# A 3x3 convolution with 2x2 maximum pooling: one five-product step becomes a four-product step, in a new written order

## The chip, the cores and the metric

The kernel runs on one core of a Trainium2 chip. The time is that of one execution on the device, in microseconds (us), as the median of several runs. TensorE multiplies, VectorE (DVE) and ScalarE (ACT) work on the accumulators, GpSimd (POOL) adds and subtracts rows in the on-chip memory, and SyncE (SP) issues loads and stores.

## The reference

The input x is 16 images of 64 channels with 64 x 64 pixels, the weight 128 x 64 x 3 x 3, all float32. The image is padded by one zero pixel on each side, convolved, and each 2 x 2 block of the result is reduced to its maximum:

```python
x_pad = np.pad(x, ((0, 0), (0, 0), (pad, pad), (pad, pad)), mode='constant')
conv[b, co] += weight[co, ci, kh, kw] * x_pad[b, ci, kh:kh+h, kw:kw+w]   # over ci, kh, kw
output[b, c, i, j] = np.max(conv[b, c, i*pool_size:(i+1)*pool_size, j*pool_size:(j+1)*pool_size])
```

The output is 16 x 128 x 32 x 32. Because only the maximum of each pair of rows is kept, the two rows of a pair may be computed with shared products.

## The kernel before

Two images are put on the 128 partitions, 64 channels each. So there are eight image pairs, and each is cut into four chunks of 16 rows: 32 steps. A step makes eight pooled rows for both images. Its two halves are called h = 0 and h = 1 (lower and upper 64 partitions); their matmuls have 64 rows each and are issued alternately, so that two run at the same time.

A step is of one of two kinds, set by the string SEQ.

- A K step works on bf16 rows (tile kx). It has five products of three matmuls each (one for each column of the filter): PAa and PAb for the even row of a pair in one accumulator, PBa and PBb for the odd row in another, and PR, the middle filter row over the sum of both rows (tile ks, made on VectorE by the entry KS), which is common to both. After PAb, ScalarE copies the first accumulator out (EV), VectorE takes the maximum into the second (MX), PR is added after that, ScalarE copies the odd columns out (OD), and VectorE takes the maximum with the even columns (CM). Its rows arrive as bf16 by a casting load on GpSimd's queue (entries L0 to L5, two steps each). The first two K steps are loaded in float32 instead (kfirst and ksecond) and cast on VectorE (XO, XE) and ScalarE (X1, X2).
- A W step works on float32 rows (tile wx, loaded by SyncE, entries LD.i). It has four products on combinations of rows: we (entry E on VectorE or e on GpSimd), wz (Z, GpSimd), wy (Y, GpSimd) and ws (S, VectorE), used by P2, P0, P3 and P1. P2 makes an accumulator, ScalarE writes its negative into a second one (SE), P0 adds to the first and P3 to the second; then copy (ev), maximum (mx), P1, and od and cm as above.

A K step so has 30 matmuls and a W step 24. Before, there are 14 K steps and 18 W steps.

The order of all of it is written out by hand in the string ORDER, one token for each instruction group, and the engines take their instructions in that order. A token such as P2.0.0+P0.1.1 (a product entry) issues the three matmuls of two products alternately. The accumulators are four banks for each half, given out first come, first served (`take`). A sum on GpSimd is made to wait for the last sum on VectorE that stands before it in ORDER (`on_gpsimd`). At the start, the weights are combined into 28 slots (D2, D0, GM, GP on VectorE, g0 to g2 copies on ScalarE, GS on GpSimd), transposed by TensorE in groups of four (TD2 and so on, line 174) and copied out (VD2 and so on, lines 185 to 191). TGM, TGP and their copies VGM, VGP serve the W steps. The first use of a bank that held transposed weights needs a matmul with zeros (line 155).

SyncE issues loads and stores in order; a store waits for its cm or CM. The last two steps in SEQ are stored by halves, the others whole.

Of the kernel before, what the change touches and what calls it, by code (L numbers as in the profile page):

```python
# [11 lines left out]
def kernel(  # L12
# [295 lines left out]
    stored = {}  # L308

    def colmax(c, i, h):  # L310
        g = (c, i, h)
# [3 lines left out]
        nc.vector.tensor_tensor(  # L315
            out=o[:, h], in0=acc[h][tb[g]][:, :, 0::2], in1=od.pop(g), op=MAX
        )
# [4 lines left out]
        n = order_of.index((c, i))
        stored[c, i] = stored.get((c, i), 0) + 1
        if n >= len(order_of) - 2:
            nc.sync.dma_start(out=dst[:, h], in_=src[:, h])
# [53 lines left out]


    ORDER = """
        D2 g0 D0 g1 TD2 KX2 g2 TD0 GS VD2 TG0 TG2 VG0 TG1 XO VD0 VG2 PAa.0.0+PAa.0.1 GM XE PAb.0.0+PAb.0.1
# [4 lines left out]
        SE.1.0 Y.1 P1.0.0+P0.1.1 MX.1.1 P0.1.0+P1.0.1 MX.1.0 ev.1.1 P3.1.0+P3.1.1 KS.2 ev.1.0 KS.3
        PR.1.0+PAa.2.1 od.0.0 mx.1.1 Z.2 PAa.2.0+PR.1.1 cm.0.0 OD.1.0 od.0.1 CM.1.0 PAb.2.0+P1.1.1 OD.1.1
        cm.0.1 PBa.2.0+PAb.2.1 E.2 od.1.1 EV.2.0 LD.5 S.2 PBb.2.0+PAa.3.1 EV.2.1 e.3 cm.1.1 PAa.3.0+PAb.3.1
        MX.2.0 PAb.3.0+PBa.2.1 mx.1.0 Y.2 P2.2.0+PBb.2.1 CM.1.1 EV.3.0 P1.1.0+P2.2.1 EV.3.1 S.3 SE.2.0  # L390
        PR.2.0+PBa.3.1 Y.3 MX.2.1 SE.2.1 P0.2.0+PBb.3.1 od.1.0 OD.2.0 cm.1.0 P3.2.0+P0.2.1 ev.2.0 Z.3 CM.2.0
        P2.3.0+PR.2.1 mx.2.0 ev.2.1 PBa.3.0+P3.2.1 MX.3.1 OD.2.1 e.4 SE.3.0 P1.2.0+P2.3.1 CM.2.1 mx.2.1
        PBb.3.0+PR.3.1 Y.4 SE.3.1 LD.6 P0.3.0+P1.2.1 MX.3.0 OD.3.1 LD.7 P3.3.0+P3.3.1 CM.3.1 ev.3.0 KS.4
        PR.3.0+P0.3.1 od.2.0 S.4 L2 od.2.1 PAa.4.0+PAa.4.1 cm.2.0 Z.5 OD.3.0 cm.2.1 ev.3.1 PAb.4.0+PAb.4.1
        mx.3.0 P2.4.0+P2.4.1 LD.8 CM.3.0 Z.4 EV.4.0 mx.3.1 P1.3.0+PBa.4.1 EV.4.1 SE.4.0 PBa.4.0+PBb.4.1 E.5
        SE.4.1 P0.4.0+P1.3.1 S.5 od.3.0 PBb.4.0+P0.4.1 Y.5 cm.3.0 ev.4.0 MX.4.1 P2.5.0+P3.4.1 od.3.1 MX.4.0
        ev.4.1 e.6 P3.4.0+PR.4.1 SE.5.0 cm.3.1 mx.4.1 PR.4.0+P2.5.1 OD.4.1 Z.6 LD.9 CM.4.1 P0.5.0+PAa.5.1
        OD.4.0 mx.4.0 SE.5.1 P3.5.0+PAb.5.1 CM.4.0 ev.5.0 KS.5 P1.4.0+P3.5.1 S.7 LD.10 PAa.5.0+P0.5.1 od.4.0
        mx.5.0 Z.7 EV.5.1 PAb.5.0+P1.4.1 ev.5.1 P1.5.0+P2.6.1 od.4.1 e.7 cm.4.1 PAa.6.0+PBa.5.1 od.5.0
        cm.4.0 SE.6.1 PAb.6.0+PBb.5.1 mx.5.1 Y.6 EV.5.0 P2.6.0+P0.6.1 EV.6.0 MX.5.1 PBa.6.0+P1.5.1 cm.5.0  # L400
        ev.6.1 S.8 PBa.5.0+PR.5.1 od.5.1 S.6 SE.6.0 PBb.6.0+PAa.6.1 cm.5.1 L3 PBb.5.0+PAb.6.1 KS.6 MX.6.0
        Y.8 P3.6.0+P2.7.1 EV.6.1 MX.5.0 P0.6.0+P3.6.1 OD.5.1 CM.5.1 e.8 PR.6.0+PBa.6.1 ev.6.0 mx.6.1
        PR.5.0+PBb.6.1 SE.7.1 mx.6.0 Y.7 OD.6.0 P2.7.0+P1.6.1 OD.5.0 CM.6.0 P1.6.0+P0.7.1 CM.5.0 SE.7.0
        MX.6.1 e.9 PAa.7.0+P3.7.1 od.6.1 LD.11 ev.7.1 P0.7.0+PR.6.1 od.6.0 mx.7.1 Y.9 PAb.7.0+PAa.7.1 OD.6.1
        cm.6.0 ev.7.0 CM.6.1 P3.7.0+PAb.7.1 KS.7 EV.7.0 P2.8.0+P1.7.1 Z.8 EV.7.1 mx.7.0 PBa.7.0+P2.8.1
        cm.6.1 od.7.1 SE.8.0 cm.7.1 P1.7.0+PBa.7.1 E.10 SE.8.1 LD.12 PBb.7.0+PBb.7.1 od.7.0 KS.8
        P0.8.0+P0.8.1 Z.10 MX.7.0 P3.8.0+P2.10.1 cm.7.0 ev.8.0 MX.7.1 P2.9.0+P3.8.1 ev.8.1 Z.9 mx.8.0
        PR.7.0+PR.7.1 SE.10.1 mx.8.1 SE.9.0 P1.8.0+P0.10.1 Y.10 OD.7.1 OD.7.0 P0.9.0+P1.8.1 CM.7.1 ev.10.1
        CM.7.0 P3.9.0+P2.9.1 S.9 od.8.1 ev.9.0 PAa.8.0+PAa.8.1 cm.8.1 L4 od.8.0 mx.9.0 SE.9.1
        PAb.8.0+PAb.8.1 e.11 cm.8.0 P2.10.0+P3.10.1 EV.8.1 P1.9.0+P0.9.1 EV.8.0 S.10 LD.13 LD.14  # L410
        PBa.8.0+P3.9.1 mx.10.1 SE.10.0 Z.11 LD.15 od.9.0 PBb.8.0+PBa.8.1 ev.9.1 cm.9.0 P0.10.0+P1.10.1 e.12
        mx.9.1 P3.10.0+P2.11.1 MX.8.0 od.10.1 ev.10.0 P2.11.0+PBb.8.1 Y.11 cm.10.1 mx.10.0 SE.11.1
        PR.8.0+P1.9.1 SE.11.0 S.11 P1.10.0+P0.11.1 OD.8.0 MX.8.1 P3.11.0+P3.11.1 Z.12 ev.11.1 CM.8.0
        P0.11.0+PR.8.1 od.9.1 mx.11.1 od.10.0 Y.12 PAa.10.0+P2.12.1 cm.10.0 OD.8.1 ev.11.0 cm.9.1
        PAb.10.0+P1.11.1 CM.8.1 mx.11.0 PBa.10.0+PAa.10.1 od.11.1 EV.10.0 S.12 PAa.9.0+PAa.9.1 LD.16 cm.11.1
        PAb.9.0+PAb.9.1 KS.9 KS.10 PBa.9.0+PAb.10.1 L5 KS.11 EV.9.1 E.13 PBb.9.0+PBa.10.1 EV.9.0 S.13
        EV.10.1 P1.11.0+PBa.9.1 MX.9.0 Y.13 P2.12.0+PBb.10.1 od.11.0 SE.12.1 cm.11.0 PBb.10.0+PBb.9.1
        MX.10.1 SE.12.0 Z.13 PR.9.0+P0.12.1 LD.17 MX.9.1 P0.12.0+P3.12.1 ev.12.1 MX.10.0 e.14 P3.12.0+PR.9.1
        ev.12.0 mx.12.1 PR.10.0+PR.10.1 OD.9.0 mx.12.0 Y.14 OD.9.1 P2.13.0+P1.12.1 CM.9.1 OD.10.0 OD.10.1
        CM.9.0 P1.12.0+P2.14.1 CM.10.0 od.12.1 Z.14 cm.12.1 PAa.11.0+PAa.11.1 od.12.0 CM.10.1 SE.14.1  # L420
        PAb.11.0+PAb.11.1 cm.12.0 SE.13.0 E.15 PBa.11.0+P2.13.1 EV.11.1 S.14 PBb.11.0+P0.14.1 EV.11.0 e.16
        SE.13.1 P0.13.0+P3.14.1 MX.11.0 ev.14.1 P2.14.0+P0.13.1 ev.13.0 Y.16 mx.14.1 P3.13.0+PBa.11.1
        SE.14.0 PR.11.0+PBb.11.1 mx.13.0 Z.15 P0.14.0+P1.14.1 MX.11.1 OD.11.0 ev.13.1 P3.14.0+P3.13.1
        CM.11.0 Z.16 od.14.1 ev.14.0 P1.13.0+P2.16.1 cm.14.1 mx.13.1 PAa.12.0+PR.11.1 Y.15 od.13.0 mx.14.0
        SE.16.1 P2.15.0+P1.13.1 OD.11.1 cm.13.0 P1.14.0+P0.16.1 CM.11.1 od.13.1 SE.15.0 cm.13.1
        PAb.12.0+PAa.12.1 S.15 ev.16.1 P0.15.0+P2.15.1 EV.12.0 E.17 P3.15.0+P3.16.1 od.14.0 SE.15.1 cm.14.0
        PAa.13.0+PAb.12.1 S.17 PBa.12.0+P0.15.1 mx.16.1 EV.12.1 ev.15.0 PBb.12.0+P3.15.1 KS.12 S.16 ev.15.1
        PAb.13.0+PBa.12.1 mx.15.0 Z.17 P2.16.0+PBb.12.1 EV.13.0 MX.12.0 P1.15.0+P1.16.1 SE.16.0 mx.15.1
        PR.12.0+PAa.13.1 MX.12.1 od.15.0 P0.16.0+PAb.13.1 cm.15.0 OD.12.0 od.16.1 CM.12.0 P3.16.0+P1.15.1
        ev.16.0 cm.16.1 P2.17.0+PR.12.1 KS.13 EV.13.1 mx.16.0 Y.17 od.15.1 PBa.13.0+P2.17.1 OD.12.1 SE.17.0  # L430
        CM.12.1 PBb.13.0+PBa.13.1 cm.15.1 SE.17.1 P0.17.0+PBb.13.1 MX.13.0 P3.17.0+P0.17.1 ev.17.0 MX.13.1
# [59 lines left out]
```

## Time and profile before

| What | Value |
|---|---|
| Median of 3 runs | 107.14 us (106.98 to 107.2) |
| The profiled execution | 106.75 us, span 105.0 us |
| TensorE busy | 99.1 us, 888 matmuls |
| VectorE busy | 89.4 us, 179 instructions |
| ScalarE busy | 78.5 us, 173 instructions |
| GpSimd busy | 63.3 us, 73 instructions |
| Read and written | 17.14 MB and 8.39 MB, 243 GB/s over the span |

The span goes from the first to the last instruction of the program on the core. The chain that ended last follows the waits back from the end, and so tells which engine's work set the time. A group is all instructions of one line, engine and shape, with the count, the busy time, the mean duration in ns, and the idle time of the engine just before them. An engine that runs one instruction into the next starts them closer together than their durations, so that counting starts is better than adding durations.

### The profile page before, as it was taken

The numbers are of one execution on the slowest core, as the hardware profiler recorded it, in microseconds if no ns is written. First come the engines' busy times: TensorE is split into PE (matmuls) and PEld (weight loads), VectorE is DVE, ScalarE is ACT, GpSimd is POOL, SyncE is SP. The second block draws the span as 40 slices with busy tenths as digits, with TensorE's granted clock in tenths as the row PEclk, the third lists the DMA queues.
The fourth block names the chain that finished last, engine by engine and source line by source line (L and its number), as shares of the span: only waits on it lengthen the run. The fifth ranks groups of instructions, "written<-read, shape, count | busy, mean of one in ns | idle before, by whom it ended". The sixth has DMA issues, their size and how long they took to land.

```text
span 105.0 us, 2492 instructions
## 1 busy us (share of the span) xinstructions
PE 99.1 (94%) x888; PEld 53.7 (51%) x889; DVE 89.4 (85%) x179; ACT 78.5 (75%) x173; POOL 63.3 (60%) x73
## 2 busy tenths in 40 slices
...
GB/s 66 363 211 198 312 197 253 261 268 301 116 167 250 256 360 373 361 151 176 197 271 228 146 153 300 414 289 134 264 372 327 45 0 180 126 0 6 200 194 106
DMA packets 12637, 22.55 MB, mean 215 GB/s; under 512 B 976, under 2 KB 9168, under 8 KB 12624
## 3 DMA queue, kind: packets, MB, share of 16 engines
...
q0 software_dynamic: 864, 3.15, 19.0%
q8 instruction: 7, 0.11, 0.5%
...
HBM read 17.14 MB, written 8.39 MB: 243 GB/s over the span
## 4 chain that ended last, share of the span: by engine, by line
PE 94%; ACT 1%; issue 0%; DVE 0%; DVEq 0%
PE acc L213 89%; PE acc L438 3%; PE acc L174 2%; ACT wt L185 1%; DVE o L315 0%; ACT od L306 0%; DVEq L486 0%
## 5 line engine op out<-in xcount | busy, mean ns | idle before, releaser
L213 PEld LDWEIGHTS <-wt 64*128 64x128 bf16 x852 | 50.3, 94 | 42.2 <-issue 1.5
L213 PE MATMUL acc<-kx,wt 64*128 64x512 bf16 (+3 forms) x336 | 54.7, 373 | 0.3 <-issue 0.3
L302 DVE TENSOR_TENSOR acc<-acc,ev 128x512 f32<-128x512 f32 x64 | 42.5, 692 | 3.4 <-ACT ev L293 1.6
L293 ACT COPY ev<-acc 128x512 f32<-128x512 f32 x64 | 35.6, 594 | 9.8 <-PE acc L213 9.5
L263 POOL TENSOR_TENSOR wz<-wx 128x512 bf16<-128x512 f32 x18 | 22.7, 1271 | 16.9 <-DVE we L263 6.1
L263 POOL TENSOR_TENSOR wy<-wx 128x512 bf16<-128x512 f32 x18 | 22.9, 1272 | 10.4 <-DVE ws L263 6.0
L306 ACT COPY od<-acc 128x256 f32<-128x256 f32 x64 | 23.0, 379 | 7.0 <-PE acc L213 6.7
L315 DVE TENSOR_TENSOR o<-acc,od 128x256 f32<-128x256 f32 x64 | 25.1, 417 | 3.2 <-ACT od L306 2.6
L213 PE MATMUL acc<-ws,wt 64*128 64x504 bf16 (+1 forms) x108 | 26.9, 377 | 0.0
L213 PE MATMUL acc<-wz,wt 64*128 64x504 bf16 (+1 forms) x108 | 26.8, 377 | 0.0
L213 PE MATMUL acc<-we,wt 64*128 64x504 bf16 (+1 forms) x108 | 26.1, 377 | 0.5 <-ACT wt L185 0.5
L213 PE MATMUL acc<-wy,wt 64*128 64x504 bf16 (+1 forms) x108 | 24.3, 377 | 0.0
L298 ACT ACTIVATE acc<-acc 128x512 f32<-128x512 f32 x36 | 20.6, 590 | 2.2 <-PE acc L213 1.8
L213 PE MATMUL acc<-ks,wt 64*128 64x504 bf16 (+1 forms) x84 | 18.8, 377 | 0.0
L263 POOL TENSOR_TENSOR we<-wx 128x512 bf16<-128x512 f32 x10 | 12.7, 1269 | 3.4 <-DVE ws L263 2.9
L263 DVE TENSOR_TENSOR ws<-wx 128x512 bf16<-128x512 f32 x18 | 13.5, 752 | 0.0
L263 DVE TENSOR_TENSOR we<-wx 128x512 bf16<-128x512 f32 x8 | 5.8, 728 | 2.1 <-DMA wx<-in_x_dram 2.1
L263 DVE TENSOR_TENSOR ks<-kx 128x512 bf16<-128x512 bf16 x14 | 5.7, 421 | 0.0
L438 PE MATMUL acc<-const-bfloat16-1.0 128*128 128x512 bf16 x8 | 3.6, 625 | 0.8 <-PEq L472 0.8
L108 POOL DMA_DIRECT2D kx<-in_x_dram x6 | 3.6, 594 | 0.0
L174 PEld LDWEIGHTS <-wq 128*128 128x128 bf16 x28 | 2.3, 124 | 1.3 <-issue 1.2
L174 PE MATMUL acc<-ident,wq 128*128 128x128 bf16 x28 | 2.7, 271 | 0.0
(27 smaller groups left out, 15.1 us busy)
## 6 DMA issues: line engine op xcount, KB each, us to landing
...
wx<-in_x_dram SPq DMA_DIRECT2D x8, 512.0 KB, 6.1
wx<-in_x_dram SPq DMA_DIRECT2D x5, 480.0 KB, 6.4
wx<-in_x_dram SPq DMA_DIRECT2D x4, 544.0 KB, 6.7
...
kfirst<-in_x_dram SPq DMA_DIRECT2D x1, 544.0 KB, 4.2
```

Source lines behind the costliest of these rows:

```text
L108: nc.gpsimd.dma_start(out=ktile(i)[:, lo:hi, :], in_=rows_of(p, lo, hi))
L174: nc.tensor.transpose(tp[:, (j - lo) * 128 : (j - lo + 1) * 128], wq[:, j : j + 2, :].rearrange("a b c -> a (b c)"), ident,)
L185: nc.scalar.mul(dst, src, 0.5)
L213: lambda kw=kw, o0=o0, o1=o1, c0=c0, c1=c1: nc.tensor.matmul(dst[:, i0:i1, o0:o1], wt[lo : lo + CI, m0 + kw - h, :], rows(lo, i0, i1, c0, c1),
L263: return engine.tensor_tensor(out=r, in0=t[:, f + a : f + a + 2 * R - 1 : 2, :], in1=t[:, f + b : f + b + 2 * R - 1 : 2, :], op=op,)
L293: nc.scalar.copy(out=ev[g], in_=acc[g[2]][ta[g]])
L298: nc.scalar.mul(acc[h][t], acc[h][ta["w", i, h]], -1.0)
L302: nc.vector.tensor_tensor(out=t, in0=t, in1=ev.pop(g), op=MAX)
L306: nc.scalar.copy(out=od[g], in_=acc[g[2]][tb[g]][:, :, 1::2])
L315: nc.vector.tensor_tensor(out=o[:, h], in0=acc[h][tb[g]][:, :, 0::2], in1=od.pop(g), op=MAX)
L438: warm = nc.tensor.matmul(acc[n % 2][n // 2], ones[:, 0:128], ones, start=True, stop=True, skip_group_check=True)
```

## The change

One K step becomes a W step: SEQ has 13 K and 19 W steps. ORDER is written out anew from the first token to the last. Casting load L0 gets an explicit wait on the first K sum (KS.0) and stands further back. In the last stretch, the first half-store that is issued after ScalarE's last EV, OD or SE goes out on ScalarE's queue. The mark for KS and the counting of ScalarE's tokens serve these two.

```diff
-    SEQ = "KWKWKWKWKWWKWKWWKWKWWKWKWKWKWWKW"
+    SEQ = "KWKWKWKWWKWKWWKWWKWKWWKWWKWKWWKW"
...
-        nc.gpsimd.dma_start(out=ktile(i)[:, lo:hi, :], in_=rows_of(p, lo, hi))
+        return nc.gpsimd.dma_start(out=ktile(i)[:, lo:hi, :], in_=rows_of(p, lo, hi))
...
         if n >= len(order_of) - 2:
-            nc.sync.dma_start(out=dst[:, h], in_=src[:, h])
+            use_act = act_left[0] == 0 and not stored["act"]
+            stored["act"] |= use_act
+            queue = nc.scalar if use_act else nc.sync
+            queue.dma_start(out=dst[:, h], in_=src[:, h])
...
     def load_k(n):
-        kload(2 * n + 2, min(2, NK - 2 * n - 2))
+        inst = kload(2 * n + 2, min(2, NK - 2 * n - 2))
+        if n == 0:
+            behind(inst, mark["KS0"])
...
-        D2 g0 D0 g1 TD2 KX2 g2 TD0 GS VD2 TG0 TG2 VG0 TG1 XO VD0 VG2 PAa.0.0+PAa.0.1 GM XE PAb.0.0+PAb.0.1
-        LD.1 GP PBa.0.0+PBa.0.1 VG1 EV.0.1 L0 KS.0 PBb.0.0+PBb.0.1 EV.0.0 E.0 TGM MX.0.1 TGP Z.0 LD.2 VGM
-        MX.0.0 X1 P2.0.0+P2.0.1 VGP Y.0 PR.0.0+PR.0.1 SE.0.0 PAa.1.0+PAa.1.1 OD.0.0 S.0 SE.0.1
-        P0.0.0+PAb.1.1 E.1 OD.0.1 X2 P3.0.0+P0.0.1 CM.0.1 LD.3 Z.1 ev.0.0 CM.0.0 PAb.1.0+P3.0.1 EV.1.1
+        D2 g2 D0 g0 TD2 KX2 g1 TD0 GS VD2 TG0 TG1 VG0 XO TG2 VD0 PAa.0.0+PAa.0.1 VG2 GM GP PAb.0.0+PAb.0.1
+        LD.1 XE TGM TGP KS.0 VGM PBa.0.0+PBa.0.1 E.0 EV.0.0 PBb.0.0+PBb.0.1 Y.0 VG1 LD.2 EV.0.1
+        P2.0.0+P2.0.1 MX.0.0 X1 L0 S.0 X2 PR.0.0+PAa.1.1 Z.0 VGP SE.0.1 PAa.1.0+PAb.1.1 MX.0.1 OD.0.0 SE.0.0
+        PAb.1.0+P3.0.1 E.1 EV.1.1 P0.0.0+P0.0.1 EV.1.0 S.1 LD.3 P3.0.0+PR.0.1 ev.0.0 KS.1 Z.1 CM.0.0
...
+        mx.13.1 od.12.0 PR.9.0+PBb.9.1 cm.12.1 ev.13.0 Y.15 cm.12.0 P3.13.0+P1.13.1 MX.9.1 OD.9.0
+        PAa.11.0+PAa.11.1 LD.17 Z.14 mx.13.0 od.13.1 P2.14.0+PR.9.1 CM.9.0 cm.13.1 PAb.11.0+PAb.11.1 S.15
+        SE.14.0 P1.13.0+PAa.10.1 OD.9.1 S.14 EV.11.1 P0.14.0+PAb.10.1 E.15 od.13.0 EV.11.0 P3.14.0+PBa.11.1
+        KS.10 ev.14.0 L5 CM.9.1 P2.15.0+PBb.11.1 cm.13.0 EV.10.1 Z.15 mx.14.0 PAa.10.0+P2.14.1 LD.18
+        PAb.10.0+PBa.10.1 S.17 SE.14.1 PBa.10.0+PBb.10.1 KS.11 EV.10.0 MX.11.1 e.17 PBb.10.0+P0.14.1 SE.15.0
...
-        P1.16.0+P3.17.1 mx.17.0 ev.17.1 PR.13.0+PR.13.1 od.16.0 mx.17.1 cm.16.0 OD.13.1 P1.17.0+P1.17.1
-        OD.13.0 CM.13.1 CM.13.0 od.17.1 od.17.0 cm.17.1 cm.17.0
+        MX.12.0 P3.18.0+P0.18.1 mx.17.1 ev.18.0 P1.16.0+P3.18.1 mx.18.0 ev.18.1 PR.12.0+P1.17.1 mx.18.1
+        od.16.0 OD.12.1 cm.16.0 od.17.1 P1.18.0+P1.18.1 OD.12.0 CM.12.1 cm.17.1 od.18.1 CM.12.0 od.18.0
+        cm.18.1 cm.18.0
...
+    def on_act(s):
+        return s.split(".")[0].upper() in ("EV", "OD", "SE")
+
+    act_left[0] = sum(map(on_act, ORDER.split()))
     for s in ORDER.split():
+        act_left[0] -= on_act(s)
```

More of the change, by code (lines that the diff above doesn't have):

```diff
@@ L270, in ks @@
     def ks(i):
-        on_vector(row_op(nc.vector, "ks", i, 0, 1, ADD))
+        return on_vector(row_op(nc.vector, "ks", i, 0, 1, ADD))
     def ws(i):
@@ L306, in odd @@
         nc.scalar.copy(out=od[g], in_=acc[g[2]][tb[g]][:, :, 1::2])
-    stored = {}
+    stored = {"act": False}
+    act_left = [0]
     def colmax(c, i, h):
@@ L387 @@
[L387 to L431, printed above, removed]
```

43 lines of the change are left out of this document (41 added, 2 removed).

## The prediction

> **What bounds the kernel now.** I read the chain that ended last first, then two places of TensorE's timeline, the busy time over the steady stage, the costliest groups, and at last the DMA answers for single stretches. Of the chain (start, length, what; us):
>
> ```profile
> 6.34 2.62 PE acc L213 x24
> 8.96 0.34 PE acc L174 x4
> 9.32 0.61 ACT wt L185
> 9.98 1.47 PE acc L213 x12
> 11.70 88.09 PE acc L213 x809
> 99.81 0.82 PE acc L213 x5
> 101.06 0.42 DVE o L315
> ```
>
> From 11.70 to the end the chain is TensorE alone. Two starts of the timeline give its pace:
>
> ```profile
> 18.86 0.38 PE L213 MATMUL acc<-ks,wt 64*128 64x512 bf16 x1
> 98.77 0.83 PE L213 MATMUL acc<-ks,wt 64*128 64x512 bf16 x6
> ```
>
> The first is the 17th product entry of the written order (PR.1.0+PAa.2.1), the second the 141st: 124 entries in 79.91 us, 0.644 us each. An entry is six matmuls that run two by two, so 0.215 us a pair. At that pace the sixteen entries before 18.86, which begin at 6.27, would take 10.3 us; they take 12.59. So 2.3 us of waiting lie in the head, and hardly any between 18.86 and 98.77. Is there room on the other engines for the steady stage to stay full?
>
> ```profile
> 18.80:98.80 80.00, 80.00 (x749) 44.75 (x746) 74.14 (x148) 64.47 (x146) 54.41 (x46) 1.00 0.74 216
> ```
>
> (PE, weight loads, VectorE, ScalarE, GpSimd; clock 1.00 throughout.) VectorE has 6 us to spare in 80, ScalarE 15, GpSimd 25. What one head wait hangs on:
>
> ```profile
> 13.87 0.69 DVE L263 TENSOR_TENSOR we<-wx 128x512 bf16<-128x512 f32 x1 [2.06 <-DMA wx<-in_x_dram]
> ```
>
> E.1 waits 2.06 us for load LD.1. What held that load is in the DMA answer for 10 to 11 us (queue, packets, MB, share of the 16 engines):
>
> ```profile
> q0 software_dynamic: 52, 0.21, 103.0%
> q1 hardware_dynamic: 2, 0.01, 2.1%
> ```
>
> The casting load L0 (GpSimd's queue) has the engines to itself while SyncE's loads stand still.
>
> **The change, part by part.**
>
> *One K step becomes a W step.* A K step is 15 pairs of matmuls, a W step 12. One of 142 entries goes: -0.64 us where TensorE is full. On the others, by the groups:
>
> ```profile
> L302 DVE TENSOR_TENSOR acc<-acc,ev 128x512 f32<-128x512 f32 x64 | 42.5, 692 | 3.4 <-ACT ev L293 1.6
> L298 ACT ACTIVATE acc<-acc 128x512 f32<-128x512 f32 x36 | 20.6, 590 | 2.2 <-PE acc L213 1.8
> L263 DVE TENSOR_TENSOR ws<-wx 128x512 bf16<-128x512 f32 x18 | 13.5, 752 | 0.0
> L263 DVE TENSOR_TENSOR ks<-kx 128x512 bf16<-128x512 bf16 x14 | 5.7, 421 | 0.0
> L263 POOL TENSOR_TENSOR wz<-wx 128x512 bf16<-128x512 f32 x18 | 22.7, 1271 | 16.9 <-DVE we L263 6.1
> ```
>
> VectorE gains one ws (0.75) and loses one ks (0.42): +0.33, since E stands on it eight times in both. ScalarE gains two seeds, 2 x 0.59 = +1.18. GpSimd gains Z, Y and e, 3 x 1.27 = +3.8. All fit into the room above; if the cover were gone, VectorE's +0.33 is the first that would show.
>
> *The head, walked by rows.* Transposes and the first two entries are as before (6.27, 6.93). Then TGM and TGP come at once; VectorE now does GP (6.46 to 6.94) ahead of XE, so both are ready. The eight transposes cost some 0.65 (the timeline has them from 8.89, 0.62 long), and PBa, PBb, P2.0 follow at about 8.14, 8.79, 9.44. The scaled copy VGM (0.60 on ScalarE) now lies beside PBa, about 8.0 to 8.6, where before P2.0 waited for it until 9.98. The fifth entry so comes 0.54 earlier. The sixth (PR.0.0+PAa.1.1) waits for MX.0.0, which can't start before PBb ends at 9.6: 9.7 to 10.4, so 10.45 (before 10.64). PAa.1.1 needs X1, which needs load ksecond; that landed at 10.2 beside L0. With L0 out of its way I take it as in time. The seventh at 11.1; the zeroing matmul costs the same 0.42 as before (11.28 to 11.70); the eighth at 12.17; the ninth waits 0.15 for SE.0.0 (12.33 to 12.91), 12.96. From there every input is early: E.1 behind MX.0.1 at 11.9 if LD.1 has landed. Eight entries on, the 17th is at 18.1, against 18.86: -0.74. Bounds: if ksecond still lands at 10.2, X1 ends at 10.85 and 0.43 of it is lost, -0.31; if both waits that are left vanish (0.36 and 0.15), -1.25. I take -0.74, the walk itself.
>
> *L0 behind the first K sum.* In the queue of GpSimd it now stands behind GS and Y.0, so it issues at about 9.6 instead of 5.37, and Z.0 waits 0.6 for that issue (594 ns mean of the six) but is wanted only at 12.9. Its landing took 7.7 before, casting loads 6.2 to 9.5 as a whole: 15.8 to 19.1. KS.3 and PAa.2.1 want it at 19.4. What it frees is LD.1: that no longer loses the 10-to-11 stretch, and its 13.85 becomes some 11, so the 2.06 wait goes, and with it 0.3 us of TensorE's small waits at 14.6 and 15.4, which the walk contains.
>
> *The steady stage.* I laid the queues of VectorE, ScalarE and GpSimd, in the new order and with the starts from one to the next that the trace shows (0.60 for a 128x512 maximum, 0.33 for a column maximum, 0.48 for a copy, 1.23 on GpSimd), beside entries at 0.644. The smallest margins are -0.04 (P2.5.0's bank, after ev.3.0), -0.03 and +0.01; the old order so laid has -0.02, where the trace shows no wait. Cost nothing. One source of delay is not in that: ws on VectorE against a running GpSimd sum,
>
> ```profile
> 23.89 1.31 DVE L263 TENSOR_TENSOR ws<-wx 128x512 bf16<-128x512 f32 x1
> 23.37 1.29 POOL L263 TENSOR_TENSOR wy<-wx 128x512 bf16<-128x512 f32 x1
> ```
>
> 1.31 instead of 0.68: it ends 0.55 after GpSimd's. In the new order S.2, S.5 and S.6 meet only the last 0.1 to 0.4 of one; margins there are larger: nothing.
>
> *Late loads.* SyncE's queue is in order. Between issue and first use the old order leaves 7 us or more; the new one leaves 6.2 once (LD.4, S.4) and 4.7 once: LD.17 stands behind the store of cm.12.0, issue about 75.7, and S.17 is up on VectorE at 80.4. Behind S.17 wait KS.11 and MX.11.1, and PR.11.1 on TensorE for that; its margin is 0.5. So a landing up to 5.2 us after issue is free, and each us beyond is a us of the time. Rows, each from the answer for the stretch of that issue (54.2; 28.9 and 29.5; 74.5):
>
> ```profile
> wx<-in_x_dram SPq DMA_DIRECT2D x1, 544.0 KB, 5.2
> ...
> wx<-in_x_dram SPq DMA_DIRECT2D x1, 512.0 KB, 5.8
> wx<-in_x_dram SPq DMA_DIRECT2D x1, 480.0 KB, 6.4
> ...
> wx<-in_x_dram SPq DMA_DIRECT2D x1, 480.0 KB, 7.8
> ```
>
> The first had a store just ahead and no casting load near; the second and third had one issued 1.3 and 0.7 after them; the last was issued while one was in flight. LD.17 has a store 0.5 ahead, and L5 (one step now, 17 rows) issues about 1.3 after it. All loads lie between 4.6 and 9.0: stall 0 to 3.8. Nearest are 5.2 and 5.8; I take 5.5, +0.3. LD.4 has a limit of 6.6 and no casting load within 3 us behind it: nothing.
> L5's own work: six casting loads take 19.0% of 105 us, 3.3 us of all engines each; L5, with 17 rows instead of 31 to 33, some 1.8. If the two ran side by side, LD.17 would lose up to half of that, 0.9: landing at 6.1 to 6.4, which is the second rival below.
> The Trainium skill (DMA: Bandwidth & Descriptors, Queues, rings and completion order) says that each DMA engine goes round-robin, packet by packet, between the queues that have work. By that rule the second rival would be the likeliest; the 103% to 2.1% above speaks against such sharing, since the queue that came first held the engines.
>
> *The end.* Last maximum, last products and five late stores stand as before: mx.18.1 waits for P3.18.1 as mx.17.1 did, and P1.18.1 again waits about 0.39 for it (99.42 to 99.81).
>
> ```profile
> 100.57 1.93 SPq L325 DMA_DIRECT2D out_dram<-o  x4
> ```
>
> SyncE's stores go 0.50 apart. The new order has six in the last stretch, one of them on ScalarE, which is done by then: five on SyncE, the last at the same distance from the last matmul. Without that move +0.50. No row has a store on ScalarE's queue; between no cost and 0.17 (a quiet store's 2.65 to landing, issued at 101.55, against the end of landings at 104.03). I take 0.
>
> **Sum.** -0.64 - 0.74 + 0.3 = -1.08 on the profiled execution: span 105.0, 106.75 with what lies around it, to 105.67. That execution is 0.39 under the median of the runs, 107.14; so 106.05.
>
> **The rivals.**
> *The late load takes it all, and more (slower).* LD.17 is shut out behind L5 as LD.1 was behind L0, or meets a queue as full as at 74.5. At 7.8 the stall is 2.6: 108.3. The gain is gone at a landing of 6.6, slower begins at 6.85; five of the fifteen loads after 14 us took over 6.6. Against it: all of those were issued with a casting load in flight or together with one, and L4 should be through. 0.19, at 106.95 to 108.3 or so.
> *The load is late by a little.* LD.17 and L5 share the engines: 6.1 to 6.4, stall 0.9 to 1.2, 106.65 to 106.95; with 6.0 to 6.8 as its edges 106.5 to 107.3. For it: both are in flight from 77 us. Against it: the stretch at 10 us. 0.15, half of it within the noise.
> *The head gains less.* ksecond at 10.2, or L0 after 19.4 so that KS.3 holds VectorE: -0.31 instead of -0.74, 106.5. 0.11.
> *As forecast,* 105.4 to 106.5: 0.55.
>
> **How the numbers follow.** Range 105.4 (both head waits gone or no stall) to 107.7 (the slower rival's middle), about 0.8. The likeliest case's own range is 105.4 to 106.5. A measurement tells about 0.2% (0.21 us). Faster: 0.55 + 0.11 + half of 0.15 = 0.74; same 0.07; slower 0.19.
>
> **What would show it.** TensorE's 17th entry at 18.1; E.1 no longer waiting for a DMA; no matmul gap from there to S.17's place, 81 to 83 us; VectorE's wait at S.17 named as a DMA wait of 0.5 to 1.2 us (0.5 of it free); the last matmul near 99.5. I am wrong if that wait is over 2 us, if L0 ends KS.3's wait, or if gaps lie elsewhere in the steady stage: then the margins were mis-laid.

## The result, and the profile after

The changed kernel takes 106.5 us (median of 5 runs, 105.98 to 107.8) against 107.14 (106.98 to 107.39): ratio 0.9941, interval 0.9916 to 0.9966. The 107.8 is a slow execution, and slow ones are left out of this ratio and of those below. The forecast was 106.05, faster. A second series gave 106.39 against 106.95, ratio 0.9937 (0.9906 to 0.9968). The profiled execution takes 106.5 us, span 104.7. So the change gained about 0.6 of the 1.08 us that the sum had.

The chain that ended last, of the kernel after (start, length, what; us):

```profile
1.17 4.67 DMA kfirst<-in_x_dram
...
6.34 1.39 PE acc L213 x12
7.74 0.55 PE acc L174 x8
8.29 1.45 PE acc L213 x12
...
9.81 0.71 DVE acc L302
...
10.56 1.47 PE acc L213 x12
12.03 0.32 PE acc L155
12.35 86.01 PE acc L213 x785
...
99.06 1.82 DVE o L316 x5
```

The wait for the scaled copy (ACT wt L185 in the chain of before) is gone, since the eight transposes (L174) now stand ahead of the first PBa. In its place the chain begins with the landing of kfirst, which sets the first product entry, and waits once for a maximum (9.81). From 12.35 to 98.36 it is TensorE alone again; the last column maxima on VectorE (99.06) stand at its end.

What held E.1 in before is gone too. Its line on VectorE's timeline, and the one queue that has packets from 10 to 11 us (packets, MB, share of the 16 engines), of after:

```profile
11.95 1.12 DVE L263 TENSOR_TENSOR we<-wx 128x512 bf16<-128x512 f32 x1
```

```profile
q1 hardware_dynamic: 52, 0.20, 68.4%
```

No wait for a DMA, and no casting load in that stretch: SyncE's loads have the engines. (The 1.12 is another matter, of which below: GpSimd's Z.0 runs beside it.)

TensorE's 17th product entry on its timeline, and the busy time from it to the start of the last entry (PE, weight loads, VectorE, ScalarE, GpSimd, each with its instructions; then clock, share of the 16 DMA engines, of which 1 is all of them full, and GB/s):

```profile
18.22 0.38 PE L213 MATMUL acc<-we,wt 64*128 64x512 bf16 x1
```

```profile
18.22:98.64 80.42, 80.42 (x746) 49.22 (x744) 74.36 (x146) 66.52 (x147) 57.94 (x50) 1.00 0.78 218
```

The 17th entry comes 0.64 sooner (18.86 before). But from there to the start of the last entry (98.64 after, 99.42 before) it takes 80.42 us against 80.56: one entry of 0.644 less, and only 0.14 gained. Where do the other 0.5 us go? The busy time doesn't tell, since a short wait between matmuls disappears in it. The starts do. VectorE's timeline at S.17, and TensorE's behind it:

```profile
81.67 0.69 DVE L263 TENSOR_TENSOR ws<-wx 128x512 bf16<-128x512 f32 x1 [0.76 <-DMA wx<-in_x_dram]
```

```profile
83.01 0.38 PE L213 MATMUL acc<-ws,wt 64*128 64x512 bf16 x1
83.36 0.37 PE L213 MATMUL acc<-ks,wt 64*128 64x512 bf16 x1
83.36 0.39 PE L213 MATMUL acc<-ws,wt 64*128 64x504 bf16 x1
```

The next matmul of the ws product is due 0.215 after 83.01, and starts 0.35 after. Here and just behind it 0.21 us are lost, and the two halves run 0.17 apart from then on. A second place is at S.8. VectorE, GpSimd and TensorE there:

```profile
49.06 1.01 DVE L263 TENSOR_TENSOR ws<-wx 128x512 bf16<-128x512 f32 x1
...
51.79 0.58 DVE L263 TENSOR_TENSOR ks<-kx 128x512 bf16<-128x512 bf16 x1
```

```profile
48.26 1.26 POOL L263 TENSOR_TENSOR we<-wx 128x512 bf16<-128x512 f32 x1 [1.32 <-PE acc L213]
50.82 1.27 POOL L263 TENSOR_TENSOR wz<-wx 128x512 bf16<-128x512 f32 x1 [1.30 <-DVE we L263]
```

```profile
53.04 0.38 PE L213 MATMUL acc<-ks,wt 64*128 64x504 bf16 x1
53.35 0.82 PE L213 MATMUL acc<-we,wt 64*128 64x512 bf16 x6
```

S.8 begins while GpSimd's e.10 runs and takes 1.01 instead of 0.68; KS.7 takes 0.58 instead of 0.41 beside Z.9. All that VectorE does behind them is later, and P2.9, which needs the bank that cm.7.0 on VectorE gives back, starts 0.18 late. A third place, at 33.8 us, has another cause. ScalarE and TensorE there:

```profile
32.67 1.07 ACT L293 COPY ev<-acc 128x512 f32<-128x512 f32 x2 [0.35 <-PE acc L213]
```

```profile
33.79 0.82 PE L213 MATMUL acc<-we,wt 64*128 64x512 bf16 x6
```

The second of these copies is ev.3.0, which ends at 33.74 and gives back the bank that P2.5.0 takes: P2.5 starts 0.10 late. S.6 on VectorE takes 0.97 just before (beside Y.5), but no matmul waits for it. And 0.06 is lost at 18.9, where P1.1.0 starts behind the maximum mx.1.0.

Last, the end. The share of the DMA engines over 2.5 us that begin 0.5 after the last matmul, first after, then before:

```profile
100.50:103.00 2.50, 0.00 (x0) 0.00 (x0) 0.71 (x2) 0.20 (x1) 0.00 (x0) 1.00 1.08 377
```

```profile
101.10:103.60 2.50, 0.00 (x0) 0.00 (x0) 0.71 (x2) 0.20 (x1) 0.00 (x0) 1.00 0.87 304
```

and the stores issued there, again after and before (count, size, median us to landing):

```profile
out_dram<-o SPq DMA_DIRECT2D x2, 256.0 KB, 2.3
out_dram<-o SPq DMA_DIRECT2D x3, 128.0 KB, 2.3
out_dram<-o ACTq DMA_DIRECT2D x1, 128.0 KB, 2.4
```

```profile
out_dram<-o SPq DMA_DIRECT2D x4, 128.0 KB, 2.0
out_dram<-o SPq DMA_DIRECT2D x1, 256.0 KB, 2.1
```

From the end of the last matmul to the end of the span it is 4.72 us after and 4.37 before. The new order ends more steps late: 1024 KB instead of 768 KB, with the engines full.

The budget of the two profiled executions: first entry +0.07, from it to the 17th -0.71, one entry -0.64, lateness behind the 17th +0.50, the halves apart at the last entry +0.17, the end +0.35. Sum -0.26; the spans differ by 0.25.

### The profile page after: what moved, and what is told of

It reads as the page before. It is cut to its first block, busy times and chain, and to the rows that moved or that the text cites. A ratio compares the mean times of both kernels' runs of the same rounds, so it can differ in the third digit from the quotient of the medians.

```text
span 104.7 us, 2487 instructions
## 1 busy us (share of the span) xinstructions
PE 98.2 (94%) x883; PEld 57.1 (54%) x883; DVE 90.0 (86%) x179; ACT 80.3 (77%) x175; POOL 67.1 (64%) x76
## 4 chain that ended last, share of the span: by engine, by line
PE 87%; DMA 4%; DVE 3%; issue 1%; SPq 0%; DVEq 0%
PE acc L213 86%; DMA kfirst<-in_x_dram 4%; DVE o L316 2%; DVE acc L302 1%; PE acc L174 1%; DVE kx L335 0%; SPq L121 0%; DVEq L497 0%; PE acc L155 0%; DVEq L302 0%
## 5 line engine op out<-in xcount | busy, mean ns | idle before, releaser
L213 PEld LDWEIGHTS <-wt 64*128 64x128 bf16 x846 | 54.2, 94 | 38.5 <-issue 2.8
L213 PE MATMUL acc<-kx,wt 64*128 64x504 bf16 (+3 forms) x312 | 59.7, 373 | 0.6 <-DVE kx L335 0.6
L213 PE MATMUL acc<-wy,wt 64*128 64x504 bf16 (+1 forms) x114 | 29.8, 377 | 0.0
L213 PE MATMUL acc<-wz,wt 64*128 64x504 bf16 (+1 forms) x114 | 29.4, 377 | 0.0
L263 POOL TENSOR_TENSOR wz<-wx 128x512 bf16<-128x512 f32 x19 | 24.2, 1275 | 7.7 <-DVE ks L263 4.1
L213 PE MATMUL acc<-ws,wt 64*128 64x504 bf16 (+1 forms) x114 | 28.7, 377 | 0.2 <-DVE acc L302 0.2
L213 PE MATMUL acc<-we,wt 64*128 64x504 bf16 (+1 forms) x114 | 27.5, 377 | 0.0
L298 ACT ACTIVATE acc<-acc 128x512 f32<-128x512 f32 x38 | 22.1, 587 | 4.4 <-PE acc L213 2.9
L213 PE MATMUL acc<-ks,wt 64*128 64x504 bf16 (+1 forms) x78 | 20.7, 376 | 0.2 <-DVE acc L302 0.2
L263 POOL TENSOR_TENSOR we<-wx 128x512 bf16<-128x512 f32 x11 | 14.0, 1275 | 8.6 <-DVE ws L263 4.6
L174 PEld LDWEIGHTS <-wq 128*128 128x128 bf16 x28 | 1.7, 102 | 1.2 <-issue 0.7
```

Of the source, the lines that this page charges most:

```text
L174: nc.tensor.transpose(tp[:, (j - lo) * 128 : (j - lo + 1) * 128], wq[:, j : j + 2, :].rearrange("a b c -> a (b c)"), ident,)
L213: lambda kw=kw, o0=o0, o1=o1, c0=c0, c1=c1: nc.tensor.matmul(dst[:, i0:i1, o0:o1], wt[lo : lo + CI, m0 + kw - h, :], rows(lo, i0, i1, c0, c1),
L263: return engine.tensor_tensor(out=r, in0=t[:, f + a : f + a + 2 * R - 1 : 2, :], in1=t[:, f + b : f + b + 2 * R - 1 : 2, :], op=op,)
L298: nc.scalar.mul(acc[h][t], acc[h][ta["w", i, h]], -1.0)
```

## The experiments

Each series had its own runs of the kernel before on the same chip, so medians compare within a series, and ratios across them. after_again, a_ld17_early, a_all_sync and a_l0_first are one (106.95 for before); a_tg_late, b_l0_wait, a_e10_later and b_drop_product the next (107.03); then c_old_seq_head, c_old_seq_head_store and a_two_act (107.17); and a_half_stores (107.02). The table is what the verdicts rest on: from each profiled execution the first product entry, the time from it to the 17th, and from the 17th to the end of the span (us); and the times of all runs.

| Kernel | First | To 17th | To the end | Median us (lowest to highest) | Ratio to before (95%) |
|---|---|---|---|---|---|
| before | 6.27 | 12.59 | 86.12 | 107.14 (106.98 to 107.39) | |
| after | 6.34 | 11.88 | 86.51 | 106.5 (105.98 to 107.8) | 0.9941 (0.9916 to 0.9966) |
| after_again | 5.79 | 11.87 | 86.14 | 106.39 (105.57 to 107.1) | 0.9937 (0.9906 to 0.9968) |
| a_ld17_early | 6.29 | 11.88 | 86.16 | 106.19 (105.76 to 106.59) | 0.9934 (0.991 to 0.9958) |
| a_all_sync | 5.92 | 12.10 | 86.42 | 106.3 (106.18 to 107.83) | 0.9962 (0.9933 to 0.9991) |
| a_l0_first | 7.46 | 11.88 | 86.52 | 107.63 (107.54 to 107.83) | 1.007 (1.0056 to 1.0085) |
| a_tg_late | 6.11 | 12.36 | 86.14 | 106.69 (106.29 to 107.53) | 0.9978 (0.9947 to 1.0008) |
| b_l0_wait | 6.21 | 12.19 | 86.13 | 106.24 (105.86 to 106.35) | 0.9914 (0.9884 to 0.9945) |
| a_e10_later | 5.81 | 11.87 | 86.78 | 107.09 (106.31 to 107.57) | 0.9991 (0.9963 to 1.002) |
| b_drop_product | 6.49 | 13.04 | 86.10 | 107.12 (106.69 to 107.54) | 1.0003 (0.9983 to 1.0024) |
| c_old_seq_head | 5.92 | 11.94 | 86.14 | 106.14 (105.85 to 106.95) | 0.9916 (0.9892 to 0.994) |
| c_old_seq_head_store | 6.23 | 11.95 | 85.89 | 105.84 (105.49 to 106.21) | 0.988 (0.9849 to 0.991) |
| a_two_act | 6.89 | 11.88 | 86.16 | 106.37 (105.7 to 107.2) | 0.9923 (0.9893 to 0.9953) |
| a_half_stores | 6.81 | 11.87 | 86.23 | 106.26 (105.93 to 106.8) | 0.993 (0.9907 to 0.9954) |

**The late load.** after_again is the kernel after, unchanged. a_ld17_early moves one token:

> The changed kernel once more, to stand beside the next three on the same chip. Expected 106.5 us again (0.994 of the time before), with VectorE waiting 0.5 to 1.2 us for load LD.17 at S.17 and a gap of TensorE of some 0.2 to 0.4 us behind that. If landings of loads vary from run to run, its runs spread by 1 us, where the kernel before spreads by 0.4.

```diff
-        P3.12.0+P2.13.1 od.11.0 ev.12.0 mx.12.1 Y.13 P2.13.0+PAb.9.1 SE.13.1 cm.11.0 PBa.9.0+P1.12.1 mx.12.0
+        P3.12.0+P2.13.1 od.11.0 ev.12.0 mx.12.1 Y.13 P2.13.0+PAb.9.1 SE.13.1 cm.11.0 LD.17 PBa.9.0+P1.12.1 mx.12.0
...
-        PAa.11.0+PAa.11.1 LD.17 Z.14 mx.13.0 od.13.1 P2.14.0+PR.9.1 CM.9.0 cm.13.1 PAb.11.0+PAb.11.1 S.15
+        PAa.11.0+PAa.11.1 Z.14 mx.13.0 od.13.1 P2.14.0+PR.9.1 CM.9.0 cm.13.1 PAb.11.0+PAb.11.1 S.15
```

> LD.17 stands ahead of the store of cm.12.0 instead of behind it, and so issues at about 72.7 instead of 76.1 us. Theory (the late load costs what TensorE loses at 83 us): S.17 no longer waits for a DMA, the two halves' matmul streams stay together to the end, and the profiled span is 0.4 shorter (104.3, with 0.25 from the gap and 0.17 from the last entry). Rival (VectorE or GpSimd is late there anyway, the load only the last to come): the wait goes, but the gap stays within 0.1, span 104.6 to 104.8.

Issued at 72.6 instead of 76.1, LD.17 has landed when S.17 comes up. VectorE's timeline of a_ld17_early:

```profile
80.80 0.78 DVE L263 TENSOR_TENSOR ws<-wx 128x512 bf16<-128x512 f32 x1
```

No wait, no gap at 83, and the halves stay together: 86.16 from the 17th entry to the end, 0.35 less than in after. (That its span is 104.3, as the theory said, is chance: after_again, without the edit, has 103.8 since it begins 0.5 earlier.) That the wait made both the gap and the skew is shown. But in after_again the load, at its old place, landed 4.5 us after its issue (5.57 in after), and the expected wait was not there either: 86.14. Of the six profiles with LD.17 at its place, three show the wait (0.76, 0.75 and 0.51, landings of 5.3 to 5.6) and three don't (4.4 to 4.5). So the term is a draw that costs 0 to 0.35 from one execution to the next. The runs do spread by 1.5 us (before by 1.3, or by 0.45 without one run of 108.0), but the start, of which below, can do that alone. The medians of the two can't be told apart. Nor is the early place safe: the same load took 5.6 us here, but 8.0 in both later kernels that have it there (a_two_act and a_half_stores), where it landed at about 81.2, just in time.

**The head, part by part.** First L0 at its old place in the new order, right behind GS and without its wait:

```diff
-            behind(inst, mark["KS0"])
+            pass
...
-        D2 g2 D0 g0 TD2 KX2 g1 TD0 GS VD2 TG0 TG1 VG0 XO TG2 VD0 PAa.0.0+PAa.0.1 VG2 GM GP PAb.0.0+PAb.0.1
+        D2 g2 D0 g0 TD2 KX2 g1 TD0 GS L0 VD2 TG0 TG1 VG0 XO TG2 VD0 PAa.0.0+PAa.0.1 VG2 GM GP PAb.0.0+PAb.0.1
...
-        P2.0.0+P2.0.1 MX.0.0 X1 L0 S.0 X2 PR.0.0+PAa.1.1 Z.0 VGP SE.0.1 PAa.1.0+PAb.1.1 MX.0.1 OD.0.0 SE.0.0
+        P2.0.0+P2.0.1 MX.0.0 X1 S.0 X2 PR.0.0+PAa.1.1 Z.0 VGP SE.0.1 PAa.1.0+PAb.1.1 MX.0.1 OD.0.0 SE.0.0
```

> Casting load L0 without its wait and straight behind GS in GpSimd's queue, so that it issues at about 5.4 as in the kernel before; the rest of the new order as it is. Theory (L0 held the DMA engines while LD.1 and ksecond stood still): ksecond lands at about 10.2 instead of 9.2, LD.1 at 13.8 instead of 11.6, E.1 waits for a DMA again, TensorE's 17th entry comes at 18.6 to 19.0 instead of 18.2, span +0.4 to +0.8. Rival (the head is shorter for the placing of the transposes and of VGM alone): 17th entry within 0.15 of 18.2, span the same.

It is 1.2 us slower than after_again, but not where the head was thought to wait: from the first to the 17th entry it takes the same 11.88. The whole head begins later, since kfirst lands 5.8 us after its issue. VectorE's cast of it:

```profile
6.98 0.43 DVE L335 CAST kx<-kfirst 128x512 bf16<-128x512 f32 x1 [1.71 <-DMA kfirst<-in_x_dram]
```

E.1 does wait for LD.1 again, 0.64 us, but this run doesn't tell what that wait costs: with a head that begins 1.1 later, LD.1 was that much less late for it. So each part was tried alone. a_tg_late puts the transposes TGM and TGP and their copy VGM back behind PBb, all else as after:

```diff
-        LD.1 XE TGM TGP KS.0 VGM PBa.0.0+PBa.0.1 E.0 EV.0.0 PBb.0.0+PBb.0.1 Y.0 VG1 LD.2 EV.0.1
+        LD.1 XE KS.0 PBa.0.0+PBa.0.1 E.0 EV.0.0 PBb.0.0+PBb.0.1 TGM TGP Y.0 VG1 LD.2 EV.0.1 VGM
```

> The kernel after with TGM and TGP behind PBb.0.0+PBb.0.1 and VGM behind EV.0.1 again, as the kernel before has them; L0 stays where the change put it. If the place of these transposes is what the head gained, P2.0 waits for VGM behind both copies of EV (P2.0 some 3.7 to 3.9 us after the first product entry, 3.2 in after), and from the first to the 17th product entry it takes 12.4 to 12.6 us, against 11.88 in after and 12.59 in before; the span grows by 0.5 to 0.7. If the gain hangs on the loads (L0 out of the way of LD.1 and ksecond), or the later waits of the head absorb the 0.6, it stays at 11.9 to 12.05 and the span with it.

TensorE's timeline at P2.0:

```profile
9.07 0.62 PE L174 MATMUL acc<-ident,wq 128*128 128x128 bf16 x8
10.16 0.82 PE L213 MATMUL acc<-we,wt 64*128 64x512 bf16 x6 [0.47 <-ACT wt L185]
```

The wait of before for ACT wt L185 is back, with the same 0.47, and the head takes 12.36 instead of 11.88 (just under the 12.4 expected): 0.48 for the place of the transposes. b_l0_wait is the other part, in the kernel before:

```diff
-        kload(2 * n + 2, min(2, NK - 2 * n - 2))
+        inst = kload(2 * n + 2, min(2, NK - 2 * n - 2))
+        if n == 0:
+            behind(inst, mark["KS0"])
...
-        LD.1 GP PBa.0.0+PBa.0.1 VG1 EV.0.1 L0 KS.0 PBb.0.0+PBb.0.1 EV.0.0 E.0 TGM MX.0.1 TGP Z.0 LD.2 VGM
+        LD.1 GP PBa.0.0+PBa.0.1 VG1 EV.0.1 KS.0 L0 PBb.0.0+PBb.0.1 EV.0.0 E.0 TGM MX.0.1 TGP Z.0 LD.2 VGM
```

> The kernel before with L0 alone moved behind the first K sum, and made to wait for it: issue near 8 us instead of 5.4. The prediction's step: LD.1 is freed, lands at 11 to 12 instead of 13.85, the wait of E.1 for its load (2.06 us) goes, and with it 0.3 us between the first and the 17th product entry (12.59 to 12.3). The rival, after the run with L0 first: that wait was not on TensorE's path, and 12.59 stays within 0.1, with the wait gone or not; the time is that of before within 0.15%.

LD.1 lands 4.7 us after its issue at 6.7, and E.1 waits for nothing:

```profile
wx<-in_x_dram SPq DMA_DIRECT2D x1, 512.0 KB, 4.7
```

```profile
12.13 0.68 DVE L263 TENSOR_TENSOR we<-wx 128x512 bf16<-128x512 f32 x1
```

The head takes 12.19 instead of 12.59, so the wait was on TensorE's path, for 0.40 of its 2.06. The time falls by more, 0.79 in the median (4 runs). The profile of b_drop_product (below) has the old head with LD.1 landing 7.9 us after its issue instead of 7.3, and takes 13.04; this points to heads of before that are worse than its profiled one, whose time was 0.39 under the median. Then both parts in the kernel before (the lines of b_l0_wait, and):

```diff
-        D2 g0 D0 g1 TD2 KX2 g2 TD0 GS VD2 TG0 TG2 VG0 TG1 XO VD0 VG2 PAa.0.0+PAa.0.1 GM XE PAb.0.0+PAb.0.1
-        LD.1 GP PBa.0.0+PBa.0.1 VG1 EV.0.1 L0 KS.0 PBb.0.0+PBb.0.1 EV.0.0 E.0 TGM MX.0.1 TGP Z.0 LD.2 VGM
+        D2 g0 D0 g1 TD2 KX2 g2 TD0 GS VD2 TG0 TG2 VG0 TG1 XO VD0 VG2 PAa.0.0+PAa.0.1 GM GP XE PAb.0.0+PAb.0.1
+        LD.1 TGM TGP VGM PBa.0.0+PBa.0.1 VG1 EV.0.1 KS.0 L0 PBb.0.0+PBb.0.1 EV.0.0 E.0 MX.0.1 Z.0 LD.2
```

> The kernel before (old SEQ, old order behind the head) with the head's two parts alone: L0 behind KS.0 with its wait, and GP, TGM, TGP and VGM where the new order has them, ahead of the first PBa. If the two gains add, 12.59 us from the first to the 17th product entry becomes 12.19 by the load (measured alone) less 0.48 (the transposes moved back): 11.6 to 11.9, with no lateness behind and the tail of before, 4.37; span 104.0, time 0.2 to 0.5 under that of the load alone, ratio 0.987 to 0.990. The rival: the two wait behind one another, the later waits of the head stay, 12.0 or more, ratio 0.991 to 0.993 as with the load alone.

11.94: between the two expectations. The parts give 0.65 together, not 0.88, because the next wait takes over (11.05 in the chain of the next kernel, behind two maxima on VectorE; the same with both kernels). In the times the transposes don't show beside the load: ratio 0.9916, with the load alone 0.9914. And c_old_seq_head_store has one late store on ScalarE besides:

```diff
+    last_act = ("w", 17, 1)
...
-            nc.sync.dma_start(out=dst[:, h], in_=src[:, h])
+            queue = nc.scalar if (c, i, h) == last_act else nc.sync
+            queue.dma_start(out=dst[:, h], in_=src[:, h])
```

> The same with the store of cm.17.1 on ScalarE's queue, so four late stores on SyncE: everything of the change but the K step that became a W step and the order of the steady stage. The tail (end of the last matmul to the end of the span) falls from 4.37 to 4.1 (the last store goes when cm.17.0 is done, 0.25 sooner). Against the whole change: if the entry of 0.64 counts in full, this is 0.4 to 0.6 slower than after; if the waits of the new order give it back (0.3 to 0.5 of lateness, 0.35 at the end), it is as fast as after, or faster by up to 0.3.

```profile
9.70 1.31 DVE acc L302 x2
...
11.05 88.07 PE acc L213 x815
```

It is the fastest kernel here: 105.84 us, ratio 0.988 (0.9849 to 0.991), with the old SEQ and the old steady stage. After the 17th entry it takes 85.89 us, while the new order never got under 86.14. So the K step that became a W step, with the order written for it, brought nothing: its 0.64 went into 0.30 of lateness (0.50 with the late load) and 0.35 at the end (0.58, when both have a late store on ScalarE). No run has the new SEQ without its order, so the two are not told apart.

**The steady stage.** a_e10_later takes away the overlap at S.8 by putting GpSimd's e.10 behind it:

```diff
-        SE.8.0 P3.7.0+PAb.6.1 KS.6 L3 OD.5.0 P0.8.0+P2.8.1 e.10 CM.5.0 EV.6.1 mx.7.0 PAa.7.0+P3.7.1 ev.7.1
-        LD.11 S.8 PAb.7.0+PBa.6.1 SE.8.1 LD.12 ev.8.0 E.9 P3.8.0+PBb.6.1 Z.9 mx.7.1 P1.7.0+P0.8.1 MX.6.1
+        SE.8.0 P3.7.0+PAb.6.1 KS.6 L3 OD.5.0 P0.8.0+P2.8.1 CM.5.0 EV.6.1 mx.7.0 PAa.7.0+P3.7.1 ev.7.1
+        LD.11 S.8 e.10 PAb.7.0+PBa.6.1 SE.8.1 LD.12 ev.8.0 E.9 P3.8.0+PBb.6.1 Z.9 mx.7.1 P1.7.0+P0.8.1 MX.6.1
```

> The kernel after with e.10 (GpSimd) behind S.8 in the written order, so that GpSimd's sum waits for VectorE's S.8 and does not overlap it. If the overlap is what made S.8 1.01 us long, it takes 0.68 again, the matmul gap of 0.18 to 0.20 at 53.3 us goes, and the lateness between the 17th and the last product entry falls from 0.30 (the repeat of after) by 0.2. The rival: S.8 is long for another reason, or e.10 now comes late for P1.10 or holds up Z.9, and a gap of 0.15 or more stands at 53 to 58 us all the same. In the time itself 0.2% at most.

VectorE, GpSimd and TensorE of this kernel:

```profile
48.52 0.68 DVE L263 TENSOR_TENSOR ws<-wx 128x512 bf16<-128x512 f32 x1
...
50.93 1.54 DVE L263 TENSOR_TENSOR ks<-kx 128x512 bf16<-128x512 bf16 x1
```

```profile
50.93 1.26 POOL L263 TENSOR_TENSOR wz<-wx 128x512 bf16<-128x512 f32 x1
```

```profile
53.46 0.83 PE L213 MATMUL acc<-we,wt 64*128 64x512 bf16 x6 [0.58 <-DVE o L316]
```

First the theory came in, then the rival. S.8 takes 0.68 again, so the overlap was its cause. But the lateness does not fall by 0.2: Z.9 now comes later and meets KS.7 from the first moment on: 1.54 us instead of 0.41, ending 0.28 after Z.9. The gap grows from 0.18 to 0.82, and the gain of the whole change is gone (0.9991). What S.8 showed as a loss of 0.3 is a matter of which operation meets GpSimd's sum, and for how long.

b_drop_product asks for the price of an entry: PR.7.0+PR.7.1 is left out of the kernel before.

```diff
-        PR.7.0+PR.7.1 SE.10.1 mx.8.1 SE.9.0 P1.8.0+P0.10.1 Y.10 OD.7.1 OD.7.0 P0.9.0+P1.8.1 CM.7.1 ev.10.1
+        SE.10.1 mx.8.1 SE.9.0 P1.8.0+P0.10.1 Y.10 OD.7.1 OD.7.0 P0.9.0+P1.8.1 CM.7.1 ev.10.1
```

> The kernel before without one product entry in the middle of the steady stage (PR.7.0+PR.7.1 is left out, so two K halves lack their middle filter row; everything else is issued). If TensorE alone bounds that stage, the span falls by one entry, 0.64 us (0.55 to 0.70), ratio about 0.994. The rival: VectorE at 93% busy or a bank's return takes over right behind, and less than 0.3 is gained, ratio 0.997 or more.

TensorE at that place:

```profile
58.07 0.37 PE L213 MATMUL acc<-ws,wt 64*128 64x512 bf16 x1 [0.35 <-DVE acc L302]
```

The rival was right: 86.10 instead of 86.12 from the 17th entry to the end. P1.8.0 now follows at once on what was before PR.7 and waits for the maximum mx.8.0; the entry had covered that wait. One place was tried, so this is no price for every entry; but "0.644 an entry, where TensorE is full" is not a price that holds by itself.

**The end.** a_all_sync takes the store on ScalarE back:

```diff
-            queue = nc.scalar if use_act else nc.sync
+            queue = nc.sync
```

> All late stores on SyncE again, none on ScalarE. Theory (the store on ScalarE saves one issue of 0.5 us on SyncE, but the landings then overlap and take 2.3 instead of 1.95): last issue 0.5 later, landing 0.35 faster, from the last matmul's end to the end of the span 4.8 instead of 4.7, time +0.1 to +0.2. Rival one (the saving is whole, the slow landing has another cause): 5.1 to 5.2, time +0.5. Rival two (the store on ScalarE only costs): 4.4 as in the kernel before, time -0.3.

The end takes 4.88 us (4.72 with the store on ScalarE, 4.37 before), as the theory had it: the last store is issued 2.03 us after the last matmul instead of 1.53, and lands in 1.96 instead of 2.30. With one queue, then, the sixth issue of 0.5 us is all of the longer end, and the landing is as quick as before (1.95). With two, the issue is sooner and the landing slower. a_two_act gives ScalarE two of the six, on top of the early LD.17:

```diff
+    two_act = (("k", 12, 0), ("w", 18, 0))
...
-            use_act = act_left[0] == 0 and not stored["act"]
-            stored["act"] |= use_act
-            queue = nc.scalar if use_act else nc.sync
+            queue = nc.scalar if (c, i, h) in two_act else nc.sync
...
-        od.16.0 OD.12.1 cm.16.0 od.17.1 P1.18.0+P1.18.1 OD.12.0 CM.12.1 cm.17.1 od.18.1 CM.12.0 od.18.0
+        od.16.0 OD.12.1 cm.16.0 od.17.1 P1.18.0+P1.18.1 OD.12.0 CM.12.1 cm.17.1 od.18.1 od.18.0 CM.12.0
```

> The kernel after with LD.17 ahead of the store of cm.12.0, and the stores of CM.12.0 and cm.18.0 on ScalarE's queue (od.18.0 written ahead of CM.12.0, so that no copy stands behind a store). SyncE then has four late stores and the last one goes when cm.18.0 is done, 0.3 sooner. If the 0.5 from one store to the next on SyncE is what lengthened the end, the tail falls from 4.72 to 4.35 to 4.45, and no gap stands at 83 us: the time some 0.3 under after's 106.4. The rival: landings beside one another on two queues take longer (the last one took 2.30 instead of 1.95 in after), and the tail stays at 4.6 or more.

The last store is issued when its maximum is done, at 101.43, and it doesn't help: 4.73. The stores of that stretch take longer to land instead:

```profile
out_dram<-o SPq DMA_DIRECT2D x2, 128.0 KB, 2.4
out_dram<-o ACTq DMA_DIRECT2D x2, 128.0 KB, 2.6
```

The rival was right: with two queues, issues are not what sets the end. The Trainium skill (DMA: Bandwidth & Descriptors, Issuing engines are not separate DMA queues) says that DMAs started by different engines run on the same 16 DMA engines, and that starting them from several saves only the time on the sequencer. The runs agree: the engines were full at 377 GB/s in after, and the second store on ScalarE's queue was issued 0.30 sooner and landed 0.30 slower. In c_old_seq_head_store, with 768 KB to store, the share of the same 2.5 us is lower, and one store on ScalarE does shorten the end, 4.38 to 4.14:

```profile
100.50:103.00 2.50, 0.00 (x0) 0.00 (x0) 0.63 (x2) 0.12 (x1) 0.00 (x0) 1.00 0.84 293
```

a_half_stores brings the bytes of the new order down to 768 KB (on top of the early LD.17):

```diff
-        if n >= len(order_of) - 2:
+        if n >= len(order_of) - 4:
```

> The kernel after with LD.17 ahead of the store of cm.12.0, and the last four steps stored by halves instead of the last two. The late stores stay six (five on SyncE, one on ScalarE), but carry 6 x 128 KB = 768 KB as in before, instead of 1024 KB; the other halves of W steps 16 and 17 go out some us earlier. If bytes set the end (the engines full at 370 to 385 GB/s from 100.5 to 103 us in after), 256 KB less frees up to 0.68 us and the tail falls from 4.73 to 4.1 to 4.4, down to what the last maximum allows (4.14 with the old SEQ and one store on ScalarE); the time is 0.3 to 0.6 under that of the same kernel without the halves. The rival: the number of issues and their 0.5 us on SyncE set it, and it stays at 4.65 or more. Two more issues in SyncE's queue come earlier, where loads have left.

```profile
100.50:103.00 2.50, 0.00 (x0) 0.00 (x0) 0.82 (x3) 0.31 (x2) 0.00 (x0) 0.84 0.88 309
```

The engines are no longer full, and the last landing comes 3.52 us after the last matmul instead of 3.83 (3.42 before). Yet the end takes 4.79. In after, all of SyncE's closing semaphore waits but one were over before the last landing, and the span ended 0.89 behind that. Here six more of these waits, 0.06 each, stood behind the one that the last landing released, and the span ended 1.27 behind it. So with fewer bytes the last store lands 0.31 sooner, 0.13 by its issue (1.40 us after the last matmul instead of 1.53) and 0.19 by its landing (2.11 instead of 2.30), and this was lost again in those waits; why they stand in another order was not tried. The ratio, 0.993, is that of a_ld17_early (0.9934).

## Why the prediction was right or wrong

*The total.* 106.05 was forecast and 106.5 measured, within the range of 105.4 to 107.7 and on the forecast side. That it is so near is in part luck. On the profiled executions, from which the sum was made, the span fell by 0.25 and not by 1.08; the medians differ by 0.64 because before's profiled execution was 0.39 under its median and after's is at its own. The gain is that much smaller because two terms that were taken as 0 cost 0.30 and 0.35; the rest is 0.07 of the late load over its 0.3, 0.08 of a later first entry and 0.03 of the head.

*The head, -0.74.* Right: -0.71 from the first to the 17th entry, and 11.87 or 11.88 in nearly every kernel of the new order. (Of the 2.3 us that the prediction called waiting, 0.62 is the eight transposes, which is work; the walk prices them as such.) In a_all_sync the named rival is seen in part: ksecond landed at 9.68, 3.8 us after the first entry (2.8 in after), X1 waited 0.46 for it, and the head took 12.10. The fifth entry was to come 0.54 earlier, by VGM beside PBa; it came 0.52 earlier (3.19 after the first entry instead of 3.71), and undoing it alone costs 0.48. LD.1 was forecast at some 11 and landed at 11.64; E.1's wait went. Its 0.3 on TensorE is 0.40 alone; the transposes, worth 0.48 in the new order, add only 0.25 to it in the old one (12.19 to 11.94), so the two gains overlap.

*L0's landing at 15.8 to 19.1.* It landed at 17.7, and no matmul waited for it. That the new order with L0 first begins 1.1 us later, with kfirst, was in no step.

*One entry, -0.64, and the steady stage, nothing.* The entry was counted right and the steady stage was mis-sized: +0.30 without the late load. That "gaps lie elsewhere in the steady stage" was the prediction's own sign of mis-laid margins, and such gaps came, at 18.9 (0.06), 33.8 (0.10) and 53.3 us (0.18). The one at 33.8 is its smallest margin, -0.04 (P2.5.0's bank, after ev.3.0), which it took as no cost. The one at 53.3 is an overlap with GpSimd that was not in its list ("S.2, S.5 and S.6 meet only the last 0.1 to 0.4 of one; margins there are larger: nothing"). S.6 took 0.97 and indeed delayed no matmul; S.8 and KS.7, which were not on the list, made VectorE 0.50 late, and 0.18 of that reached TensorE. The Trainium skill (SBUF — State Buffer, SBUF: two separate sides) says that a VectorE operation with two inputs from this memory and a GpSimd operation share a pair of ports that whichever starts first holds for its whole instruction, while the other is blocked. The traces agree, with a constant: in before, after, after_again and a_e10_later, each float32 sum on VectorE that met more than the last 0.1 us of a GpSimd sum ended 0.55 to 0.56 us after it, and each bf16 sum 0.28 to 0.29, be it 0.12 or 1.26 us that they met. That is 0.13 less than each takes alone (0.68 and 0.41). By that rule each overlap could have been priced by what was left of GpSimd's sum.

*The late load, +0.3.* Right for the profiled execution: landing 5.57 (5.5 forecast), VectorE's wait 0.76 (0.5 to 1.2), the gap at 83 us (81 to 83). It cost 0.21 at once and 0.17 by the skew at the end. In the repeat the landing took 4.5 and it cost nothing. The slower rival (shut out behind L5, 7.8) and the sharing rival (6.1 to 6.4) weren't seen in any profile that left LD.17 in place, where it landed in 4.4 to 5.6. So the round-robin rule of the Trainium skill that the prediction weighed gave no landing of 6.1 or more here; with L5's issue 1.4 us behind LD.17's, no run shows more of it than that. Nor is "the queue that came first held the engines" a rule: from 79 to 80 us of after, SyncE's queue had 59.6% of the engines and the casting queue 44.1%, side by side.

*The end, 0 (0 to 0.17).* Wrong, +0.35. The step was "six in the last stretch, one of them on ScalarE, ... the last at the same distance from the last matmul". The issue did come at about the same distance (1.53 after the last matmul, 1.47 before). But the second 256 KB store had been counted as one issue like the others: with these bytes on two queues the engines were full, and the last landing took 2.30 instead of 1.95 (2.11 in a_half_stores, without them; why not 1.95 stays open). "Without that move +0.50" was right: 4.88 against 4.37.
